# Work behind a rotation, scheduled behind products traced ahead, in a two-layer hybrid block

## The chip, the cores and the metric

One core of one Trainium2 chip runs the whole program. The metric is the device time of one execution in microseconds (us); the figure of a kernel is the median of its runs.

## The reference, cut to what matters

Two layers (`DEPTH = 2`) work on x of 512 tokens by 1024 features. Each layer is this, in float32:

```python
h = rms_norm(x, g_pre_mix)
proj = h @ w_in                      # q, k, v, qi, ki, wi, xr, gr, zu, zv, gate_logits
q = apply_partial_rope(q); k = apply_partial_rope(k)
qi = apply_partial_rope(qi); ki = apply_partial_rope(ki)
y_a = dsa_attention(q, k, v, qi, ki, wi)   # qi, ki, wi score the keys; each query keeps its top 128
xr = causal_depthwise_conv(xr, conv_w, conv_b)
y_b = rg_lru(xr, ...) * gelu(gr)
y_c = chunked_spatial_gating(gelu(zu), rms_norm(gelu(zv), g_gmlp_v), w_spatial, b_spatial)
merged = sum of sigmoid(gate_logits) * (y_n @ w_branch[n]) over n
x = x + rms_norm(merged @ w_out, g_post_mix)
x = x + rms_norm(square(relu(rms_norm(x, g_pre_ffn) @ w_ffn_up)) @ w_ffn_down, g_post_ffn)
x = x + rms_norm((p @ w_ple) * sigmoid(x @ w_ple_gate), g_post_ple)
```

## The kernel before

x lies transposed on the chip, as eight tiles `X0` to `X7` of 128 features by 512 tokens. Every float32 product is made of three products of a narrower type, xh·wh, xh·wl and xl·wh (`mm3`, L297; L356 for the first weights, L590 where tokens stand on the other side), so each operand is first split: a ScalarE cast gives the high part, a subtraction the low part. Weights come in pieces of 128 by 1024 (512 KB) through SyncE's DMA queue: `prep()` (L232) issues the load of `wr`, the cast to `wh` on ScalarE (L243) and the subtraction to `wl` on VectorE (L244). `wh` and `wl` have four buffers each, so a cast also waits until TensorE has done with the piece four back.

The rotation `rope()` (L571) takes a product from PSUM: a multiplication (L573) and a shuffle (L574) on VectorE, a multiplication (L575) and an addition (L576) on GpSimd. Behind it stands a split of its result: `ki_split` for the indexer's key, `stacked` (L645: cast L650 on ScalarE, subtraction L651 on VectorE) for the indexer's four queries `qi0` to `qi3` (tiles `A0` to `A7`) and later for the keys, `q_split` for the attention's queries (L1026 to L1028). `xc_split` (L615) is a split behind the convolution: a cast (L616) and a GpSimd subtraction (L617), four times in a layer (tiles `B0` to `B7`).

The order of the work comes from two places. The program is written by Python code with a clock of its own, `clk`: each product that is written moves it on (`tick`), `defer(us, fn)` writes `fn` once the clock has gone on by `us`, and queues of tasks (indexer, attention) run by it too. A scheduler then orders the instructions of each engine by what they depend on and by where they were written. On the chip each engine takes its instructions strictly in that order. `TURN` (5) is the delay of the splits behind a rotation, `ATT` that of the attention.

Layer one begins on weights that arrive: `FIRST` lists the rows of X at which the pieces of the first three weights (of `xr`, three times eight tiles, 72 products of 512 columns) are cut. Beside them the squares of x are made on ScalarE (L392) and summed into `sacc` on GpSimd (L398), the norm is finished by L408 (sum over partitions on TensorE), L427, L428 (a power on GpSimd), L434 (transposition) and L443. Right behind the 72 products stand the transpositions of the rotation's tables (L163), which need sines (L153, after a load of ScalarE's table) and eight small VectorE instructions (L159, L160). Later norms are made in two halves of 256 tokens, `row(...)`, with the same lines.

Of the kernel before, what the change touches and what calls it, by code (L numbers as in the profile page):

```python
# [12 lines left out]
AF = mybir.ActivationFunctionType  # L13
# [4 lines left out]
S = 512  # L18
D = 1024
KT = 8  # L20
# [20 lines left out]
V_PRE, V_POST, V_FFN, V_PFFN, V_PPLE = 0, 8, 16, 24, 32  # L41
# [9 lines left out]
def hybrid_block_kernel(ctx, tc, xT, pT, pos, vec, bsp, freq, w_in, w_tok, w_lru, w_sp, w_br, w_out, w_up, w_dn, w_ple, w_gate, out, depth=DEPTH, dbg=None):  # L51
    nc = tc.nc
    V, A, G, PE = nc.vector, nc.scalar, nc.gpsimd, nc.tensor
# [13 lines left out]
    def tmp(dt=F32):  # L67
        return tp.tile([128, S], dt, tag="tmp", name=nm("tmp"), bufs=NTMP)
# [11 lines left out]
    FULL = slice(0, S)  # L80
# [7 lines left out]
    TAIL = 3  # L88
    LEAD = 256
    ATT = 13  # L90
    TURN = 5
    WARM = 120
    FIRST = [0, 1, 4]

# [27 lines left out]
    X = [cp.tile([128, S], F32, tag=f"X{k}", name=f"X{k}") for k in range(KT)]  # L124
# [136 lines left out]
    def defer(us, fn):  # L261
        later.append((clk[0] + us, uid[0], fn))
        uid[0] += 1

    def run_later(force=False):
        while later:
# [5 lines left out]
    def add_task(q, gen):  # L272
        q["wait"].append(gen)
# [101 lines left out]
    sacc = cp.tile([128, S], F32, tag="sacc", name="sacc")  # L375

    class Stats:
# [23 lines left out]
        def add(self, src, r=FULL):  # L401
            self.square(src, r)
            self.accumulate(r)
# [33 lines left out]
        def row(self, div, dst):  # L437


            def complete(r):  # L440
                def tok():
                    self.rstd_tok(div, r)
                    defer(3.0, lambda: A.copy(dst[:, r], self.rstd_bc(r)))  # L443

                defer(2.2, tok)

            return complete

# [22 lines left out]
    XS = [(slot(f"xh{k}", F32R), slot(f"xl{k}", F32R)) for k in range(KT)]  # L471

    def x_tiles(r, xs, g=None, st=None, ys=None, bc=None, gp=None, on_g=()):

        def updated(d):
            if ys is not None and d < KT:
                if gp is None:
                    V.tensor_mul(ys[d][:, r], ys[d][:, r], bc)  # L480
                else:
                    V.scalar_tensor_tensor(ys[d][:, r], ys[d][:, r], gp[:, d:d + 1], bc, op0=ALU.mult, op1=ALU.mult)
                (G if d in on_g else V).tensor_add(X[d][:, r], X[d][:, r], ys[d][:, r])  # L483

        updated(0)
        for d in range(KT):
            x = X[d][:, r]
            if xs is not None:
                hi, lo = [v[:, r] for v in xs[d]]
                if g is None:  # L490
                    A.copy(hi, x)
                else:
                    A.activation(hi, x, AF.Copy, scale=g[:, d:d + 1])  # L493
                if st is not None:
                    st.square(x, r)
            updated(d + 1)
            if st is not None:
                st.accumulate(r)
            if xs is not None:
                if g is None:  # L500
                    V.tensor_sub(lo, x, f32v(hi))
                else:
                    V.scalar_tensor_tensor(lo, x, g[:, d:d + 1], f32v(hi), op0=ALU.mult, op1=ALU.subtract)  # L503
            yield d
# [28 lines left out]
    for l in range(depth):  # L533
        vc = vecs[l]
# [5 lines left out]
        if l == 0:  # L540
            st = Stats()

            def gen():
                tiles = x_tiles(FULL, XS, vc[:, V_PRE:V_PRE + 8], st)
                for k in range(KT):
                    first_parts(k)
                    yield next(tiles)

            gen0 = gen()
        else:  # L550
            st = st_next
# [4 lines left out]
        def proj(name, ahead=LA):  # L556
            ps = bank()
            gemm(ps, getw(("in", l, name), ahead), XS, KT)
            return ps
# [11 lines left out]
        def rope(ps, n=128):  # L571
            t1, u = tmp(), tmp()
            V.tensor_mul(t1[:n], ps[:n], Cr[:n])  # L573
            V.stream_shuffle(u[:n], ps[:n], mask=SHUF)  # L574
            G.tensor_mul(u[:n], u[:n], Sr[:n])  # L575
            G.tensor_add(t1[:n], t1[:n], u[:n])  # L576
            return t1
# [19 lines left out]
        idxq = {"wait": [], "act": [], "max": 1}  # L597
# [5 lines left out]
        for j in range(4):  # L603
            ps = first[j]
            xr = tmp()
            V.tensor_mul(xr, ps, R)
            xc = slot(f"M{4 + j}")
            A.activation(xc, xr, AF.Identity, bias=col(V_CB + j), scale=col(V_CW + 12 + j))
            for i in range(3):
                s = 3 - i  # L610
                V.scalar_tensor_tensor(xc[:, s:], xr[:, :S - s], col(V_CW + 4 * i + j), xc[:, s:], op0=ALU.mult, op1=ALU.add)
            xh, xl = slot(f"B{j}", F32R), slot(f"B{4 + j}", F32R)
            XC.append((xc, xh, xl))

            def xc_split(xc=xc, xh=xh, xl=xl):  # L615
                A.copy(xh, xc)  # L616
                G.tensor_sub(xl, xc, f32v(xh))  # L617

            defer(10 + 5 * j, xc_split)


        ps = proj("ki")
# [5 lines left out]
            A.copy(kih[64:128], kf[0:64])  # L628
            A.copy(kil[64:128], f32v(kil[0:64]))

        defer(TURN, ki_split)
        wf = tmp()
        A.copy(wf, ps)
        WI = small(32, "wi", 2).rearrange("p (t h) -> p t h", t=4)
# [5 lines left out]
            for t in range(1, 4):  # L640
                V.tensor_scalar(WI[:, t, :], pw[:, t * 128 + 64:t * 128 + 72], rt[:, t:t + 1], IDX_SCALE, op0=ALU.mult, op1=ALU.mult)

        defer(9, wi_turn)

        def stacked(f, q0, q1):  # L645


            for s, q in enumerate((q0, q1)):
                r, other = slice(64 * s, 64 * s + 64), slice(64 - 64 * s, 128 - 64 * s)
                A.copy(q[r], f[r])  # L650
                V.tensor_sub(q[other], f[r], f32v(q[r]))  # L651
            return q0, q1

        QI = []
        for j in range(4):
            ps = proj(f"qi{j}")
            QI.append((slot(f"A{j}", F32R), slot(f"A{4 + j}", F32R)))
            defer(TURN, lambda f=rope(ps), q=QI[j]: stacked(f, *q))

        def qk(a, b, c, d, jobs):  # L660

# [39 lines left out]
        def indexer():  # L701
            sc = {t: tmp() for t in (1, 2, 3)}
            for t in (1, 2, 3):
                yield from scores(t, sc[t])
            for t in (1, 2, 3):
                yield from select(t, sc[t])
# [23 lines left out]
            G.tensor_scalar(BIAS[t], gt[:, :n], -NEG, NEG, op0=ALU.mult, op1=ALU.add)  # L730
            yield 1.0

        defer(9, lambda: add_task(idxq, indexer()))


        bs = tmp()
# [282 lines left out]
        for j in range(4):  # L1019
            f = rope(proj(f"q{j}"))  # L1020
            q2, ql = (slot(f"A{j}", F32R), slot(f"A{4 + j}", F32R)), tmp(F32R)

            def q_split(f=f, q2=q2, ql=ql):
                for s in range(2):
                    r, other = slice(64 * s, 64 * s + 64), slice(64 - 64 * s, 128 - 64 * s)
                    A.copy(q2[s][r], f[r])  # L1026
                    V.tensor_sub(ql[r], f[r], f32v(q2[s][r]))
                    A.copy(q2[s][other], f32v(q2[s][r]))  # L1028

            defer(TURN, q_split)  # L1030
            Q.append((q2, ql))
            defer(TURN, lambda f=rope(proj(f"k{j}")), j=j: stacked(f, KK[0][:, j], KK[1][:, j]))
            if j == 0:
                finish(idxq)
            defer(ATT, lambda j=j: add_task(attq, attention(j)))
            gated(1, YB, ds=range(2 * j, 2 * j + 2))
# [206 lines left out]
```

## Time and profile before

| | |
|---|---|
| time, median of 3 runs | 1851.07 us (1850.51 to 1853.98) |
| the profiled execution | 1852.94 us, of which the span of instructions is 1851.2 us |
| TensorE (PE) busy | 1803.0 us, 97% of the span |
| VectorE (DVE) busy | 1159.5 us, 63% |
| ScalarE (ACT) busy | 800.3 us, 43% |
| GpSimd (POOL) busy | 361.6 us, 20% |
| DMA | 167.77 MB, 91 GB/s on the average |

The engines are shown as PE, DVE, ACT, POOL and SP; the profile's instruction times overlap a little, since the next instruction starts before the one ahead has quite ended. The idle time that a row gives in brackets is that of its engine just before it, with what ended it. The granted clock is a share of TensorE's full speed.

### The profile page before, as it was taken

The page shows a single profiled execution, that of the slowest core. Times are in us where ns is not written, and L with a number is a line of the kernel's source. Part 1 is how long each engine was busy: PE and PEld are TensorE (multiplying, and loading weights), DVE is VectorE, ACT ScalarE, POOL GpSimd, SP SyncE. Part 2 cuts the span into 40 slices and gives each one's busy share as a digit, 9 for nine tenths or more (in the row PEclk, how much of TensorE's full clock was granted, in tenths as well). Part 3 has the DMA queues.
Part 4 walks back from the last instruction along what each step waited for, and adds up shares of the span by engine and source line. Part 5 has one row for each costly group of instructions (what it writes and reads, how often), then busy time and mean ns, then how long its engine had stood idle before and what let it go on. Part 6 is the DMA issues. An engine that isn't in the chain of part 4 may idle for free.

```text
span 1851.2 us, 22873 instructions
## 1 busy us (share of the span) xinstructions
PE 1803.0 (97%) x8798; PEld 1507.5 (81%) x8798; DVE 1159.5 (63%) x1939; ACT 800.3 (43%) x1292; POOL 361.6 (20%) x292
## 2 busy tenths in 40 slices
PE   8899999999999999999998999999999999999997
PEld 7787887888888888888887878877888888888886
DVE  6689996666386253533685999866563852544355
ACT  5466435664453322223455573455544432222233
POOL 3513212210240000003454141222004200000033
PEclk9999999999999999999999999999999999999999
DMA  5122322222223232332212223222222222222321
GB/s 173 63 92 85 98 92 91 69 80 82 90 80 108 97 98 96 99 106 91 92 58 97 68 92 103 91 80 72 89 80 92 92 92 101 96 97 97 108 80 58
DMA packets 49678, 167.77 MB, mean 91 GB/s; under 512 B 6048, under 2 KB 8864, under 8 KB 49568
## 3 DMA queue, kind: packets, MB, share of 16 engines
q1 hardware_dynamic: 47376, 163.64, 26.8%
q10 hardware_dynamic: 2192, 2.67, 0.4%
q8 instruction: 69, 1.13, 0.3%
q14 instruction: 41, 0.34, 0.1%
HBM read 164.19 MB, written 2.10 MB: 90 GB/s over the span
## 4 chain that ended last, share of the span: by engine, by line
PE 72%; DVE 12%; POOL 6%; issue 6%; ACT 4%; DMA 0%; SPq 0%; POOLq 0%; DVEq 0%; ACTq 0%
PE ps L298 21%; PE ps L299 20%; PE ps L300 20%; PE ps L356 3%; PE ps L590 3%; DVE wl L244 2%; POOL tmp L575 1%; POOL tmp L576 1%; DVE tmp L716 1%; DVE m L714 1%; POOL sacc L398 1%; POOL X L483 1%; PE ps L681 1%; PE ps L967 1%; DVE tmp L790 1%
## 5 line engine op out<-in xcount | busy, mean ns | idle before, releaser
L243 ACT CAST wh<-wr 128x1024 fp32r<-128x1024 f32 x303 | 316.6, 1049 | 453.3 <-PE ps L300 365.9
L244 DVE TENSOR_TENSOR wl<-wr,wh 128x1024 fp32r<-128x1024 f32 x303 | 386.8, 1280 | 188.7 <-ACT wh L243 188.0
L298 PE MATMUL ps<-xh,wh 128*128 128x512 f32 (+1 forms) x1296 | 502.7, 388 | 0.9 <-DVE tmp L370 0.9
L299 PE MATMUL ps<-xh,wl 128*128 128x512 f32 (+1 forms) x1296 | 495.5, 382 | 3.0 <-DVE wl L244 3.0
L300 PE MATMUL ps<-xl,wh 128*128 128x512 f32 (+1 forms) x1296 | 495.6, 382 | 0.0
L398 POOL TENSOR_TENSOR sacc<-sacc,tmp 128x256 f32<-128x256 f32 (+1 forms) x99 | 109.8, 1109 | 894.8 <-issue 584.5
L300 PEld LDWEIGHTS ps<-xl,wh 128*128 128x128 f32 x1296 | 243.9, 188 | 48.2
L299 PEld LDWEIGHTS ps<-xh,wl 128*128 128x128 f32 x1296 | 244.4, 189 | 47.1 <-DVE wl L244 3.9
L298 PEld LDWEIGHTS ps<-xh,wh 128*128 128x128 f32 x1296 | 244.0, 188 | 47.2 <-issue 1.9
L300 PE MATMUL ps<-V,wh 128*128 128x512 f32 (+1 forms) x528 | 195.4, 370 | 0.0
L298 PE MATMUL ps<-K,wh 128*128 128x512 f32 (+1 forms) x432 | 158.2, 366 | 0.0
L299 PE MATMUL ps<-K,wl 128*128 128x512 f32 (+1 forms) x432 | 157.8, 365 | 0.0
L300 PE MATMUL ps<-B,wh 128*128 128x512 f32 x336 | 130.9, 390 | 0.0
L298 PE MATMUL ps<-A,wh 128*128 128x512 f32 x320 | 125.0, 391 | 0.2 <-ACT A L369 0.2
L299 PE MATMUL ps<-A,wl 128*128 128x512 f32 x320 | 124.6, 389 | 0.0
L1102 DVE TENSOR_TENSOR M<-M,ps 128x512 f32<-128x512 f32 x48 | 33.0, 688 | 141.4 <-PE ps L300 141.4
L300 PEld LDWEIGHTS ps<-V,wh 128*128 128x128 f32 x528 | 99.5, 188 | 16.7
L1090 DVE TENSOR_TENSOR tmp<-ps,R 128x512 f32<-128x512 f32 x64 | 43.8, 690 | 108.6 <-PE ps L300 108.5
L356 PE MATMUL ps<-xl,wh 128*128 128x256 f32 (+1 forms) x264 | 88.1, 334 | 6.2 <-DVE xl L503 5.5
L298 PEld LDWEIGHTS ps<-K,wh 128*128 128x128 f32 x432 | 81.5, 189 | 13.3
L299 PEld LDWEIGHTS ps<-K,wl 128*128 128x128 f32 x432 | 81.5, 189 | 13.1
L356 PE MATMUL ps<-xh,wh 128*128 128x256 f32 (+1 forms) x264 | 87.1, 330 | 2.2 <-ACT xh L493 2.2
(237 smaller groups left out, 2733.0 us busy)
## 6 DMA issues: line engine op xcount, KB each, us to landing
wr<-in_w_in_dram SPq DMA_DIRECT2D x95, 512.0 KB, 3.3
wr<-in_w_up_dram SPq DMA_DIRECT2D x64, 512.0 KB, 3.3
wr<-in_w_dn_dram SPq DMA_DIRECT2D x64, 512.0 KB, 3.3
wr<-in_w_br_dram SPq DMA_DIRECT2D x24, 512.0 KB, 3.3
wr<-in_w_tok_dram SPq DMA_DIRECT2D x16, 512.0 KB, 3.3
wr<-in_w_out_dram SPq DMA_DIRECT2D x16, 512.0 KB, 3.3
wr<-in_w_gate_dram SPq DMA_DIRECT2D x16, 512.0 KB, 3.3
X<-in_xT_dram SPq DMA_DIRECT2D x8, 256.0 KB, 5.9
```

The costliest lines, as they stand in the source:

```text
L243: A.copy(hi, raw)
L244: V.tensor_sub(lo, raw, f32v(hi))
L298: PE.matmul(ps, wh, xh, start=start, stop=False)
L299: PE.matmul(ps, wl, xh, start=False, stop=False)
L300: PE.matmul(ps, wh, xl, start=False, stop=stop)
L356: PE.matmul(pss[o][:, r], (h3, l3, h3)[m][:, q], xs[q][m // 2][:, r], start=q == 0 and m == 0, stop=q == KT - 1 and m == 2)
L398: G.tensor_add(sacc[:, r], sacc[:, r], self.q[r.start, r.stop])
L483: (G if d in on_g else V).tensor_add(X[d][:, r], X[d][:, r], ys[d][:, r])
L575: G.tensor_mul(u[:n], u[:n], Sr[:n])
L590: PE.matmul(ps, x, w, start=k == 0 and i == 0, stop=k == KT - 1 and i == 2)
L1090: V.tensor_mul(t, ps, R)
L1102: V.tensor_add(F[d], F[d], ps)
```

## The change

`TURN` goes from 5 to 7; the splits behind a rotation and `xc_split` are deferred through `turn_later`, which also gives each of their ScalarE, VectorE and GpSimd instructions a dependency on the TensorE instruction written last, for the scheduler alone (no wait on a semaphore comes from it). `xc_split` is deferred by 12 + 5j (10 + 5j before), `wi_turn` by 14 (9), the indexer by 12 (9), the end of a norm's first half by 8.0 (2.2). In layer one the squares are written beside the first products, and their sums in two groups of four and three. `FIRST` has one more cut, so X1 and X2 to X3 have pieces of their own (128 and 256 columns wide, in place of 384), three more loads in SyncE's queue, three more casts and three more subtractions.

```diff
-    TURN = 5
+    TURN = 7
     WARM = 120
-    FIRST = [0, 1, 4]
+    FIRST = [0, 1, 2, 4]
...
+    def behind_products(fn):
+        ins = nc.cur_bb.bb.instructions
+        n0 = len(ins)
+        mark = next(i for i in reversed(ins[:n0]) if i.engine == mybir.EngineType.PE)
+        fn()
+        for i in nc.cur_bb.bb.instructions[n0:]:
+            if i.engine in (mybir.EngineType.Activation, mybir.EngineType.DVE, mybir.EngineType.Pool):
+                tc.add_manual_dep(i, mark.name, mybir.DependencyInfo(mybir.DependencyClass.NoSync, mybir.DependencyReason.SCHED_ONLY), reason="behind products")
+
+    def turn_later(us, fn):
+        defer(us, lambda: behind_products(fn))
...
-                defer(2.2, tok)
+                defer(2.2 if r.stop == S else 8.0, tok)
...
-                tiles = x_tiles(FULL, XS, vc[:, V_PRE:V_PRE + 8], st)
+                tiles = x_tiles(FULL, XS, vc[:, V_PRE:V_PRE + 8])
+                qs = []
                 for k in range(KT):
                     first_parts(k)
-                    yield next(tiles)
+                    k = next(tiles)
+                    qs.append(tmp() if k else sacc)
+                    A.activation(qs[k], X[k], AF.Square)
+                    if k in (5, KT - 1):
+                        def add(qs=qs[1:5] if k == 5 else qs[5:]):
+                            for q in qs:
+                                G.tensor_add(sacc, sacc, q)
+                        behind_products(add)
+                    yield k
...
-            defer(10 + 5 * j, xc_split)
+            turn_later(12 + 5 * j, xc_split)
...
-        defer(TURN, ki_split)
+        turn_later(TURN, ki_split)
...
-        defer(9, wi_turn)
+        defer(14, wi_turn)
...
-            defer(TURN, lambda f=rope(ps), q=QI[j]: stacked(f, *q))
+            turn_later(TURN, lambda f=rope(ps), q=QI[j]: stacked(f, *q))
...
-        defer(9, lambda: add_task(idxq, indexer()))
+        defer(12, lambda: add_task(idxq, indexer()))
...
-            defer(TURN, q_split)
+            turn_later(TURN, q_split)
             Q.append((q2, ql))
-            defer(TURN, lambda f=rope(proj(f"k{j}")), j=j: stacked(f, KK[0][:, j], KK[1][:, j]))
+            turn_later(TURN, lambda f=rope(proj(f"k{j}")), j=j: stacked(f, KK[0][:, j], KK[1][:, j]))
```

Where instructions of an engine stand now is seen in its order. The lines of the new file are some 14 to 26 higher: L383 and L384 are L369 and L370 of before, L599 and L600 the rotation's L573 and L574, L642 is L616, L667 is L641, L676 and L677 are L650 and L651.

The first place is on VectorE in layer one, beside the indexer's queries; it stands so in layer two as well. `wl_119`, `wl_129` and `wl_138` are three weights that follow each other, `A0` and `A4` the split of the first query, `A1` and `A5` that of the second. Before:

```order
L244 TENSOR_TENSOR wl_119_654<-wr_117_651,wh_118_653 128x1024
L641 TENSOR_SCALAR wi_105_604<-ps_120_675,rt_37_283 128x8 x3
L573 TENSOR_TENSOR tmp_123_696<-ps_116_650,tmp_73_523 128x512
L651 TENSOR_TENSOR A0_111_642<-tmp_113_644,A0_111_642 64x512
L651 TENSOR_TENSOR A4_112_643<-tmp_113_644,A4_112_643 64x512
L574 STREAM_SHUFFLE tmp_124_697<-ps_116_650 128x512
L244 TENSOR_TENSOR wl_129_706<-wr_127_703,wh_128_705 128x1024
L573 TENSOR_TENSOR tmp_132_741<-ps_126_702,tmp_73_523 128x512
L574 STREAM_SHUFFLE tmp_133_742<-ps_126_702 128x512
L651 TENSOR_TENSOR A1_121_694<-tmp_123_696,A1_121_694 64x512
L651 TENSOR_TENSOR A5_122_695<-tmp_123_696,A5_122_695 64x512
L244 TENSOR_TENSOR wl_138_751<-wr_136_748,wh_137_750 128x1024
```

And after, from the same weight on (`wl_128` is the second weight here):

```order
L244 TENSOR_TENSOR wl_119_657<-wr_117_654,wh_118_656 128x1024
L384 TENSOR_TENSOR M1_102_610<-tmp_99_603,M0_101_609 64x512
L599 TENSOR_TENSOR tmp_122_692<-ps_116_653,tmp_73_532 128x512
L600 STREAM_SHUFFLE tmp_123_693<-ps_116_653 128x512
L244 TENSOR_TENSOR wl_128_702<-wr_126_699,wh_127_701 128x1024
L677 TENSOR_TENSOR A0_111_645<-tmp_113_647,A0_111_645 64x512
L677 TENSOR_TENSOR A4_112_646<-tmp_113_647,A4_112_646 64x512
L667 TENSOR_SCALAR wi_105_613<-ps_129_729,rt_37_286 128x8 x3
L599 TENSOR_TENSOR tmp_132_744<-ps_125_698,tmp_73_532 128x512
L600 STREAM_SHUFFLE tmp_133_745<-ps_125_698 128x512
L244 TENSOR_TENSOR wl_138_754<-wr_136_751,wh_137_753 128x1024
```

Each weight and each rotation now stands one split further ahead: the second weight ahead of A0 and A4, the third ahead of A1 and A5.

The second place is ScalarE in the same stretch, where the casts feed both. Before, from the last cast of `xc_split` on:

```order
L616 CAST B3_92_561<-M7_91_556 128x512
L629 CAST M1_102_601<-M1_102_601 64x512
L243 CAST wh_128_705<-wr_127_703 128x1024
L650 CAST A0_111_642<-tmp_113_644 64x512
L650 CAST A4_112_643<-tmp_113_644 64x512
L243 CAST wh_137_750<-wr_136_748 128x1024
L650 CAST A1_121_694<-tmp_123_696 64x512
L650 CAST A5_122_695<-tmp_123_696 64x512
```

And after:

```order
L243 CAST wh_127_701<-wr_126_699 128x1024
L642 CAST B1_82_552<-M5_81_547 128x512
L655 CAST M1_102_610<-M1_102_610 64x512
L676 CAST A0_111_645<-tmp_113_647 64x512
L676 CAST A4_112_646<-tmp_113_647 64x512
L243 CAST wh_137_753<-wr_136_751 128x1024
L642 CAST B2_87_561<-M6_86_556 128x512
L676 CAST A1_120_690<-tmp_122_692 64x512
L676 CAST A5_121_691<-tmp_122_692 64x512
L243 CAST wh_150_803<-wr_149_801 128x1024
```

The casts B1 to B3 of `xc_split`, which all stood ahead of the splits, now stand between them; so do their subtractions on GpSimd (L617), of which three stood ahead of the key's rotation and one does now.

The third place is ScalarE in layer one behind the arriving products: the sines for the rotation's tables and the first whole weights. Before:

```order
L243 CAST wh_50_412<-wr_49_410 128x1024
L153 ACT_TABLE_LOAD
L153 ACTIVATE tmp_60_436<-tmp_60_436 128x32 x2
L243 CAST wh_53_421<-wr_52_419 128x1024
L243 CAST wh_57_430<-wr_56_428 128x1024
L164 COPY ropeC_234<-ps_62_452 128x512
```

And after:

```order
L243 CAST wh_50_421<-wr_49_419 128x1024
L243 CAST wh_53_430<-wr_52_428 128x1024
L243 CAST wh_57_439<-wr_56_437 128x1024
L153 ACT_TABLE_LOAD
L153 ACTIVATE tmp_60_445<-tmp_60_445 128x32 x2
L243 CAST wh_67_490<-wr_66_488 128x1024
L164 COPY ropeC_234<-ps_62_461 128x512
```

The load of the table and the sines stood ahead of `wh_53` and `wh_57` and stand behind them now. Those two casts need the buffers of the first two arriving weights.

## Rows read from the trace of the kernel before

**Rows 1.** Waits of TensorE: what it waited for, us in total, times, longest us.
```profile
PE ps L590 <- DVE wl L244: 10.5, 4, 4.2
PE ps L356 <- DVE xl L503: 5.5, 9, 2.2
PE ps L299 <- DVE wl L244: 4.4, 4, 1.5
PE ps L967 <- ACT tmp L369: 4.1, 4, 2.3
...
PE ps L967 <- DVE tmp L370: 1.7, 4, 0.9
PE ps L639 <- ACT tmp L633: 1.2, 2, 0.7
```

**Rows 2.** Timeline of TensorE, layer one: start us, us, engine, line, instruction, [idle before].
```profile
72.81 0.39 PE L590 MATMUL ps<-wh,xl 128*128 128x512 f32 x1
...
74.86 0.39 PE L590 MATMUL ps<-wh,xl 128*128 128x512 f32 x1
79.46 0.80 PE L590 MATMUL ps<-wl,xh 128*128 128x512 f32 x1 [4.21 <-DVE wl L244]
...
84.23 0.40 PE L590 MATMUL ps<-wh,xl 128*128 128x512 f32 x1
```

**Rows 3.** Timeline of VectorE in the same stretch.
```profile
68.86 1.41 DVE L651 TENSOR_TENSOR A<-tmp,A 64x512 fp32r<-64x512 f32 x2 [3.45 <-ACT A L650]
...
75.38 2.76 DVE L651 TENSOR_TENSOR A<-tmp,A 64x512 fp32r<-64x512 f32 x2 [1.93 <-ACT A L650]
78.18 1.23 DVE L244 TENSOR_TENSOR wl<-wr,wh 128x1024 fp32r<-128x1024 f32 x1
```

**Rows 4.** Timeline of ScalarE in the same stretch.
```profile
68.21 1.26 ACT L650 CAST A<-tmp 64x512 fp32r<-64x512 f32 x2 [3.87 <-POOL tmp L576]
69.49 1.05 ACT L243 CAST wh<-wr 128x1024 fp32r<-128x1024 f32 x1
74.73 1.26 ACT L650 CAST A<-tmp 64x512 fp32r<-64x512 f32 x2 [4.18 <-POOL tmp L576]
```

**Rows 5.** Timeline of GpSimd in the same stretch.
```profile
59.39 1.28 POOL L576 TENSOR_TENSOR tmp<-tmp,tmp 64x512 f32<-64x512 f32 x1
...
71.00 2.33 POOL L575 TENSOR_TENSOR tmp<-tmp,tmp 128x512 f32<-128x512 f32 x1 [2.83 <-DVE tmp L574]
```

**Rows 6.** Windows: stretch, length, busy of PE, PEld, DVE, ACT, POOL, clock, DMA.
```profile
100.00:120.00 20.00, 20.00 (x93) 16.92 (x92) 16.85 (x52) 15.55 (x28) 2.12 (x2) 1.00 0.30 103
200.00:220.00 20.00, 19.34 (x86) 15.69 (x85) 19.73 (x35) 6.16 (x9) 1.29 (x1) 1.00 0.33 106
980.00:1000.00 20.00, 14.76 (x55) 11.36 (x54) 12.42 (x18) 5.80 (x8) 12.15 (x9) 0.83 0.32 104
```

**Rows 7.** Timeline of ScalarE, VectorE and TensorE, behind the arriving products.
```profile
21.62 1.28 ACT L153 ACT_TABLE_LOAD   x1
28.88 0.35 ACT L153 ACTIVATE tmp<-tmp 128x32 f32<-128x32 f32 x2 [5.97 <-DVE tmp L152]
30.70 2.00 ACT L243 CAST wh<-wr 128x1024 fp32r<-128x1024 f32 x2 [1.47 <-issue]
...
29.49 0.17 DVE L159 TENSOR_SCALAR tmp<-tmp 128x32 f32<-128x32 f32 x1
...
31.82 1.04 PE L163 MATMUL ps<-ident,tmp 128*128 128x128 f32 x8
```

**Rows 8.** Timeline of VectorE and GpSimd, beside the arriving products.
```profile
15.46 5.19 DVE L370 TENSOR_TENSOR wl<-wr,wh 128x512 fp32r<-128x512 f32 x3
...
16.99 6.47 POOL L398 TENSOR_TENSOR sacc<-sacc,tmp 128x512 f32<-128x512 f32 x4 [0.30 <-ACT tmp L392]
```

**Rows 9.** Timeline of TensorE: a norm's first half, and attention in layer two.
```profile
531.71 0.43 PE L434 MATMUL ps<-ident,rt 128*128 128x128 f32 x2 [0.37 <-POOL rt L428]
...
1212.28 1.04 PE L967 MATMUL ps<-tmp,V 128*128 128x256 f32 x4 [2.35 <-ACT tmp L369]
```

## The prediction

> **What bounds the kernel now.** TensorE does: it is busy for 97% of the span, so only what it waits for, and what it runs slowly, can be won. I read first the list of TensorE's waits [rows 1], which names the releaser and the number of times: most of what it waits for late in the program is a weight's subtraction (L244) or a cast or subtraction of the attention. Then the timelines of the four engines around the longest of these waits [rows 2 to 5], to see why the weight was late; then windows [rows 6], to see where VectorE has room to catch up and where the clock falls; then the same around the starts [rows 7, 8].
>
> In the stretch at 75 us, nine products from 72.81 to 74.86 us take 0.228 us each. The twelve steps from 74.86 to 84.23 us take 9.37 us where 2.73 would do: 6.64 us lost, 4.21 idle and 2.4 in slow steps behind it [rows 2]. In layer two's copy of it the granted clock is 0.83 over 20 us [rows 6]: part of it at the 1.2 GHz level after 4.2 idle us, the rest at 2.4. The weight that TensorE waits for was cast by 70.54 us [rows 4], but its subtraction starts at 78.18, behind the split of the second query (A1, A5), which starts at 75.38 after a wait for ScalarE [rows 3]; ScalarE had waited 4.18 us for GpSimd's addition [rows 4]. GpSimd had itself waited 2.83 us for a shuffle [rows 5], which stood on VectorE behind the first query's split, itself held up by 3.45 us [rows 3]. So work that was ready (a weight) stands behind work that was not (a rotation's end), twice in each layer.
>
> **The change, part by part.**
>
> *Splits behind a rotation.* In the new order the weight stands ahead of the split that held it. I take the times of before as a bound. The key's addition on GpSimd ends at 60.67 [rows 5]; two casts and a weight's cast later (two of 0.63, half of the pair of 1.26, and 1.05 [rows 4]) it is 63.0, so that the second weight is subtracted (1.23 [rows 3]) by about 64.3. TensorE asks for it near 71. The third weight's cast stays behind A0 and A4, at 70.54; VectorE then has only those two (until 70.27) and, as an estimate, at most 3.2 us of rotation ahead, the time in which it did as much between 70.27 and 73.45 (75.38 less its wait of 1.93) [rows 3]. It ends near 74.7. TensorE asked at 75.25 (79.46 less 4.21), now about 1 us sooner. That is a near thing by GpSimd's old times, but these improve: three of the four subtractions L617 stood ahead of the key's rotation and one does now, and the second query's shuffle comes before the second weight, some 6 us sooner. I therefore count all of it as gone, in both layers: the four waits of 10.5, the two of 1.2 for the transposition behind L633, which `wi_turn` now writes later (both [rows 1]), and twice 2.4 of slow steps: **−16.5 us**. Bounds: a fourth weight that comes late, below, gives 12 back.
>
> What is late next? VectorE is busy 16.85 of 20 us at 100 to 120, so it follows TensorE there and carries no backlog into what comes after; at 200 to 220 it is busy 19.73 [rows 6].
>
> *Later weights of the same layers.* The other four waits for weights, 4.4 us [rows 1], are two a layer, behind the indexer's queries. The new order puts the first weight there ahead of the LRU's VectorE work and defers the third behind it. VectorE's whole work stays the same, and it has next to no idle time until 220, so what is won before 200 is mostly asked for again by 220 [rows 6]. **−2.0**, bounds 0 and −4.4.
>
> *Attention.* A cast for the probabilities (L369) stood behind the splits of the next query, as at 1212.28 [rows 9], and stands ahead of them now, on both engines. These waits are 4.1 and 1.7 us in all [rows 1], and slow steps follow the longest. Some latency stays, since TensorE goes from a transposition to this product at once: **−4.5**, bounds 0 and −7.5 (5.8, and 1.7 for slow steps after a wait half as long as that of [rows 2]).
>
> *First half of a norm.* Its transposition waited 0.37 us [rows 9], once in each layer; it is written 50 to 80 products later now, and what reads it later has the second half to wait for anyway: **−0.7**, bounds −1.5 and +1.
>
> *Finer first pieces.* X1 has 384 KB less ahead of it in SyncE's queue, so TensorE's second batch of products starts sooner. But VectorE ends the stretch: it makes three subtractions in 5.19 us beside GpSimd's sums [rows 8], where the wait for `xl` then follows (the longest, 2.2 [rows 1]). Three subtractions more, a quarter of that size each, are 3 × 1.73 / 4 = 1.3 us at that rate, and their wider partners are smaller by as much. I take 0, bounds −1 and +1.3. The two groups of squares I cost at nothing: the order has the seven additions where they were, each waiting for its own square; GpSimd's idleness hides them, and a rival prices the contrary.
>
> *The sines.* This one goes the other way. ScalarE loaded its table at 21.62 and made the sines at 28.88, ahead of two weight casts that had to wait for buffers until 30.70 [rows 7]. Now the sines stand behind these casts: 30.70 + 2.00 + 1.28 + 0 puts them at 33.98. The fifth of the eight VectorE instructions began 0.61 after the sines did (29.49 less 28.88), so the table's transpositions can begin near 34.65, not 31.82 [rows 7]. Nothing else stands on TensorE in between: behind those transpositions are queued all the products of the next weight, although it is ready. +2.8, and slow steps behind an idle time of that length, between 0 and 2.4 [rows 2], of which I take 2.0, since the engine also has small transpositions there: **+4.8**, bounds +2.8 and +5.2.
>
> The table's load takes 1.28 us in that row. The Trainium skill ("ScalarE: Activation LUTs", What ACT_TABLE_LOAD costs) gives the same for the load but adds a drain of about 1.38 us to each switch of tables. By the page this term would be +6.2 and the time 1833; these rows do not show what follows a load directly, since the sines waited for VectorE.
>
> Sum: −16.5 − 2.0 − 4.5 − 0.7 + 0 + 4.8 = **−18.9**. From the profiled execution's own 1852.94 (1851.2 of span and 1.7 around it) that is 1834.0; this execution lies 1.9 above the median, so from the median of 1851.07 it is **1832**.
>
> **The rivals.**
>
> *A. A wait takes the place of the one removed.* The fourth weight's cast now stands behind A1's and A5's. By the old times these casts end at 75.99, the weight's at 77.04, and with the split (2.76) and 2.6 for a rotation and the weight itself VectorE is done at 80; TensorE would ask near 76.3, 7.9 before 84.23. That is 3.7 of wait and 2.4 of slow steps a layer, 12 in all: **1844**. For it: only GpSimd's earlier additions prevent it. Against it: the shuffle that held the additions back is now 6 us sooner.
>
> *B. VectorE becomes the bound.* If its stretch from 140 to 240 did not move forward with TensorE, the gains ahead of it would come back as waits for weights: of 16.5 + 2.0 nothing is left, −4.5 − 0.7 + 4.8 = −0.4, **1851**. For it, 19.73 busy of 20; against it, the idle time at 100 to 120 [rows 6]. Half of it gives 1841.
>
> *C. The sines cost nothing*, because the casts find their buffers earlier: 1832 − 4.8 = **1827**. Against it: the buffers are freed by the arriving products themselves, 1.1 us before the transpositions.
>
> *D. The two groups do hold the sums back.* Then VectorE is undisturbed until the sixth tile, and the wait of 2.2 and its slow steps go, about −4: **1828**. Against it: the order.
>
> *E. Slower.* GpSimd's subtractions now lie between the rotations, beside VectorE's weights. Two splits took 1.41 undisturbed and 2.76 beside GpSimd [rows 3], so a disturbed weight may cost 1.2 more. A weight feeds 24 products, 5.5 us by [rows 2], so the 120 us from 140 to 260 hold some 22. From eight more of them disturbed in each layer while VectorE is full, 19.2 are lost and the kernel is slower; with fifteen, 36, and it is at **1868**. Against it: GpSimd has as many instructions as before, and those of that stretch do not move into it. The Trainium skill speaks for the mechanism ("GPSIMD Engine Reference", 1. Specifications): GpSimd shares its SBUF interfaces with VectorE, with contention where VectorE's instruction has two SBUF inputs, as every subtraction here has. The rows agree, with the pair of 1.41 and 2.76.
>
> **How the numbers follow.** Forecast 0.53; A 0.12; B half 0.12, whole 0.06; C 0.07; D 0.05; E 0.05. Anything within 0.2% (3.7 us) cannot be told from no change. Faster: 0.53 + 0.12 + 0.12 + 0.07 + 0.05 = 0.89; same, B whole, 0.06; slower, E, 0.05. For the range I go on the good side to C with the later weights in full and half of the attention's rest (1832 − 4.8 − 2.4 − 1.5 = 1823), on the other to A: **1823 to 1844**, which leaves out B whole, E and a little beyond both ends.
>
> **What would show it.** Right: no wait of TensorE on L244's successor at 70 to 85 us and 915 us later, clock 1.00 there; a wait of about 2.8 us ahead of L163's successor near 32 us, released by VectorE behind ScalarE's sines, with slow steps after it. Wrong: a wait for the fourth weight (A), waits for weights at 177 to 240 that sum to more than 4.4 (B), L163 starting at 32 (C), GpSimd's first addition long after the first square (D), weights' subtractions longer on the mean than the 1.23 of [rows 3] in more places than before (E).

## The result: half the gain that was forecast

The changed kernel took 1840.32 us, the median of 4 runs (1838.18 to 1843.74), beside 1850.85 for the kernel before in the same runs. The ratio is 0.9941, with a 95% interval of 0.9922 to 0.9960: faster by 10.5 us, where 1832 stood in the forecast (18.9 faster). The range of 1823 to 1844 holds it. The profiled execution took 1840.19 us, of which the span is 1838.5: 12.7 less than before.

The page's busy times, and the list of TensorE's waits (what it waited for, us in total, times, longest), of the changed kernel:

```profile
PE 1799.8 (98%) x8798; PEld 1507.8 (82%) x8798; DVE 1172.6 (64%) x1942; ACT 795.6 (43%) x1291; POOL 369.2 (20%) x292
```

```profile
PE ps L313 <- DVE wl L244: 9.5, 5, 3.3
PE ps L370 <- DVE xl L518: 6.2, 10, 1.9
PE ps L616 <- DVE wl L244: 3.9, 2, 2.0
PE ps L163 <- DVE tmp L160: 2.8, 1, 2.8
```

L616 is the old L590, L313 the old L299, L370 the old L356. Beside [rows 1], the four waits of 10.5 us behind the rotation have become two of 3.9, the attention's waits (L967 before, L993 now) and that of the transposition behind `wi` (L639) are gone, and two things are worse: a wait for the sines (L163) that was not there, and waits for weights at L313 of 9.5 us where 4.4 stood.

**Where the time went.** The waits alone miss slow steps, products that TensorE starts 0.427 us apart behind a wait, at the lower clock, and not 0.227. So I took TensorE's timeline in both profiles and subtracted the start of the first product with the same weight, all along the program. The sums of this difference by stage (us; the places are times in the kernel before):

| stage | forecast, both layers | after | delay alone (e4) | indexer at 9 (e1) | also sines, fourth weight (e6) |
|---|---|---|---|---|---|
| arriving weights, to 50.45 | +4.8 | +2.19 | +0.79 | +0.16 | −3.50 |
| layer one: rotation, to 130.88 | −16.5 | −6.53 | −0.20 | −6.57 | −8.73 |
| layer one: later weights, to 231.78 | −2.0 | +4.92 | +4.98 | +0.07 | −0.03 |
| layer one: attention, to 386.98 | −4.5 | −5.69 | −1.10 | −5.71 | −5.71 |
| to 964.95 | −0.7 | +0.23 | +0.22 | +0.69 | +0.64 |
| layer two: rotation, to 1045.62 | above | −6.60 | +1.13 | −5.06 | −8.97 |
| layer two: later weights, to 1143.79 | above | +4.96 | +4.96 | +0.04 | +0.02 |
| layer two: attention, to 1302.91 | above | −6.42 | −3.32 | −5.35 | −5.38 |
| to the end | | +0.28 | +0.30 | +0.32 | +0.31 |
| sum | −18.9 | −12.66 | +7.76 | −21.41 | −31.35 |

The sums agree with the differences of the spans, one profile of each kernel. The last three columns belong to experiments below. One row is far off the wrong way: the later weights, forecast to give 2.0 in all, cost 4.9 in each layer.

**The later weights.** VectorE's timeline of the changed kernel (start us, us, engine, line, instruction, [idle before]); L895 are the LRU's subtractions (L869 before), L244 the three weights:

```profile
168.52 1.49 DVE L244 TENSOR_TENSOR wl<-wr,wh 128x1024 fp32r<-128x1024 f32 x1 [2.44 <-ACT wh L243]
172.26 1.77 DVE L895 SCALAR_TENSOR_TENSOR B<-tmp,B 128x512 f32<-128x512 f32 x1 [2.26 <-POOL tmp L894]
...
174.48 1.53 DVE L244 TENSOR_TENSOR wl<-wr,wh 128x1024 fp32r<-128x1024 f32 x1
175.93 1.53 DVE L895 SCALAR_TENSOR_TENSOR B<-tmp,B 128x512 f32<-128x512 f32 x1
...
178.50 1.66 DVE L895 SCALAR_TENSOR_TENSOR B<-tmp,B 128x512 f32<-128x512 f32 x1
...
180.56 0.67 DVE L895 SCALAR_TENSOR_TENSOR B<-tmp,B 128x512 f32<-128x512 f32 x1
...
183.52 1.22 DVE L244 TENSOR_TENSOR wl<-wr,wh 128x1024 fp32r<-128x1024 f32 x1
```

GpSimd in the same stretch:

```profile
171.18 1.04 POOL L894 TENSOR_TENSOR tmp<-B 128x512 f32<-128x512 f32 x1
...
173.44 4.92 POOL L894 TENSOR_TENSOR tmp<-B 128x512 f32<-128x512 f32 x3
```

ScalarE's casts of the second and third weight:

```profile
169.54 1.05 ACT L243 CAST wh<-wr 128x1024 fp32r<-128x1024 f32 x1
...
176.32 1.03 ACT L243 CAST wh<-wr 128x1024 fp32r<-128x1024 f32 x1
```

And TensorE, in layer one and in layer two:

```profile
181.12 0.39 PE L312 MATMUL ps<-xh,wh 128*128 128x512 f32 x1
184.79 0.80 PE L313 MATMUL ps<-xh,wl 128*128 128x512 f32 x1 [3.28 <-DVE wl L244]
...
1092.39 0.79 PE L313 MATMUL ps<-xh,wl 128*128 128x512 f32 x1 [3.28 <-DVE wl L244]
```

The second weight is cast by 170.59, while VectorE stands idle for 2.26 us until GpSimd's first L894 ends; it is subtracted at 174.48, behind the first L895. The third is cast by 177.35, on ScalarE behind activations of the LRU, and subtracted at 183.52: it stands behind all four of L895 and, between them, steps of the indexer, which VectorE works off without a pause from 172.26 on. TensorE stands still for 3.28 us from 181.5 and goes on in slow steps, 2.92 us more. The idle VectorE ahead of a ready weight is the forecast's own picture of the rotation, work that is ready behind work that is not, 100 us further on. How much of the third weight's delay is that lost time, and how much the order behind it, the runs don't separate.

**The rotation.** VectorE's timeline beside the indexer's queries, with the weights (L244) and the splits (L677):

```profile
67.19 3.37 DVE L677 TENSOR_TENSOR A<-tmp,A 64x512 fp32r<-64x512 f32 x2
...
72.24 1.81 DVE L244 TENSOR_TENSOR wl<-wr,wh 128x1024 fp32r<-128x1024 f32 x1
74.08 3.37 DVE L677 TENSOR_TENSOR A<-tmp,A 64x512 fp32r<-64x512 f32 x2
...
78.71 1.21 DVE L244 TENSOR_TENSOR wl<-wr,wh 128x1024 fp32r<-128x1024 f32 x1
```

ScalarE ahead of the last of these weights, then TensorE:

```profile
71.74 0.62 ACT L676 CAST A<-tmp 64x512 fp32r<-64x512 f32 x1 [2.35 <-POOL tmp L602]
...
73.03 1.06 ACT L243 CAST wh<-wr 128x1024 fp32r<-128x1024 f32 x1
```

```profile
79.97 0.50 PE L616 MATMUL ps<-wl,xh 128*128 128x512 f32 x1 [1.87 <-DVE wl L244]
```

The third weight is subtracted at 72.24 and TensorE no longer waits for it. The fourth (78.71) stands behind A1's and A5's split, which takes 3.37 us beside GpSimd (2.76 in [rows 3], and 1.41 for the pair that ran undisturbed there), and behind the next rotation's two instructions. Its cast was done by 74.09, so without the split in between it should have been in time; e6 below tests that. This is rival A, at a third of its price.

**The sines.** ScalarE, VectorE and TensorE behind the arriving products, which end at 28.2 (31.8 before):

```profile
26.99 2.00 ACT L243 CAST wh<-wr 128x1024 fp32r<-128x1024 f32 x2 [6.01 <-PE ps L370]
29.01 1.28 ACT L153 ACT_TABLE_LOAD   x1
30.30 0.35 ACT L153 ACTIVATE tmp<-tmp 128x32 f32<-128x32 f32 x2
```

```profile
13.99 2.98 DVE L384 TENSOR_TENSOR wl<-wr,wh 128x512 fp32r<-128x512 f32 x3
...
30.56 0.18 DVE L159 TENSOR_SCALAR tmp<-tmp 128x32 f32<-128x32 f32 x1
```

```profile
31.15 1.94 PE L163 MATMUL ps<-ident,tmp 128*128 128x128 f32 x8 [2.83 <-DVE tmp L160]
```

The wait is the one forecast, 2.83 us against 2.8, with 2.28 us of slow steps behind it. But the arriving products ended 3.7 us sooner, which the forecast had at nothing. The three subtractions of VectorE beside them took 2.98 us where they took 5.19 [rows 8].

The windows of the changed kernel (stretch, length, busy of PE, PEld, DVE, ACT, POOL, clock, DMA) show where TensorE is now at the lower of its two levels for part of the time, 1.2 GHz instead of 2.4:

```profile
30.00:40.00 10.00, 8.85 (x35) 7.56 (x36) 2.61 (x11) 2.75 (x6) 1.03 (x1) 0.66 0.53 159
70.00:90.00 20.00, 18.13 (x84) 14.81 (x83) 18.06 (x22) 10.93 (x17) 12.23 (x8) 1.00 0.21 66
175.00:195.00 20.00, 16.72 (x62) 13.30 (x61) 19.54 (x28) 11.71 (x15) 12.28 (x8) 0.83 0.25 79
970.00:1000.00 30.00, 27.98 (x128) 22.93 (x127) 25.82 (x30) 18.05 (x27) 19.70 (x12) 1.00 0.29 93
```

The rotation's stretches are at 1.00 (0.83 in layer two before [rows 6]); 175 to 195 is at 0.83 and the stretch behind the sines, from 30 to 40, at 0.66.

### The profile page after: what moved, and what is told of

The parts are those of the page before. It is cut to its first block, busy times and chain, and to the rows that moved or that the text cites. A ratio compares the mean times of both kernels' runs of the same rounds, so it can differ in the third digit from the quotient of the medians.

```text
span 1838.5 us, 22885 instructions
## 1 busy us (share of the span) xinstructions
PE 1799.8 (98%) x8798; PEld 1507.8 (82%) x8798; DVE 1172.6 (64%) x1942; ACT 795.6 (43%) x1291; POOL 369.2 (20%) x292
## 3 DMA queue, kind: packets, MB, share of 16 engines
q8 instruction: 69, 1.13, 0.3%
## 4 chain that ended last, share of the span: by engine, by line
PE 80%; DVE 8%; POOL 5%; issue 3%; ACT 3%; SPq 0%; DMA 0%; ACTq 0%; POOLq 0%; DVEq 0%
PE ps L312 23%; PE ps L314 23%; PE ps L313 23%; PE ps L616 4%; PE ps L370 3%; DVE wl L244 1%; PE ps L993 1%; DVE tmp L742 1%; PE ps L979 1%; POOL X L498 1%; DVE m L740 1%; PE ps L707 1%; POOL sacc L412 1%; POOL tmp L601 1%; DVE M L637 1%
## 5 line engine op out<-in xcount | busy, mean ns | idle before, releaser
L244 DVE TENSOR_TENSOR wl<-wr,wh 128x1024 fp32r<-128x1024 f32 x303 | 384.9, 1272 | 192.6 <-ACT wh L243 192.3
L313 PE MATMUL ps<-xh,wl 128*128 128x512 f32 (+1 forms) x1296 | 498.1, 384 | 9.5 <-DVE wl L244 9.5
L313 PEld LDWEIGHTS ps<-xh,wl 128*128 128x128 f32 x1296 | 245.7, 190 | 55.6 <-DVE wl L244 12.0
L412 POOL TENSOR_TENSOR sacc<-sacc,tmp 128x256 f32<-128x256 f32 (+1 forms) x92 | 99.2, 1078 | 884.9 <-issue 584.1
L313 PE MATMUL ps<-K,wl 128*128 128x512 f32 (+1 forms) x432 | 157.8, 365 | 0.0
L313 PE MATMUL ps<-A,wl 128*128 128x512 f32 x320 | 124.5, 389 | 0.0
L370 PE MATMUL ps<-xl,wh 128*128 128x256 f32 (+1 forms) x264 | 87.9, 333 | 6.9 <-DVE xl L518 6.2
L313 PEld LDWEIGHTS ps<-K,wl 128*128 128x128 f32 x432 | 81.5, 189 | 13.1
L370 PE MATMUL ps<-xh,wh 128*128 128x256 f32 (+1 forms) x264 | 86.0, 326 | 0.0
```

The costliest lines, as they stand in the source:

```text
L244: V.tensor_sub(lo, raw, f32v(hi))
L313: PE.matmul(ps, wl, xh, start=False, stop=False)
L370: PE.matmul(pss[o][:, r], (h3, l3, h3)[m][:, q], xs[q][m // 2][:, r], start=q == 0 and m == 0, stop=q == KT - 1 and m == 2)
L412: G.tensor_add(sacc[:, r], sacc[:, r], self.q[r.start, r.stop])
```

## The experiments

Ratios are to the kernel before in the same runs, with 95% intervals; the changed kernel stands at 0.9941. All start from the changed kernel.

**e1_idx9: the indexer's delay back at 9.**

```diff
-        defer(12, lambda: add_task(idxq, indexer()))
+        defer(9, lambda: add_task(idxq, indexer()))
```

> The changed kernel with the indexer started 9 behind the key's rotation again, as before the change, in place of 12. In the order this puts the three weights behind the LRU's first activations side by side again, where the change had put the third behind four subtractions of the LRU. Theory 1 (what stands ahead of a weight in an engine's order decides): the two waits of 3.28 us for that third weight, the slow steps behind them and the wait of 1.49 us in layer two go, and at most the 1.5 and 0.7 us a layer of the kernel before are left there; some 8 to 10 us less, 1831. Theory 2 (VectorE is full from 140 to 240 us and asks back what TensorE won at 70 to 85): waits for weights in that stretch still sum to over 9 us, wherever they stand, and the time stays at 1838 to 1842.

Measured: 1832.4 us (1831.44 to 1835.2), ratio 0.9896 [0.9881, 0.9911]. VectorE's timeline:

```profile
166.94 1.75 DVE L895 SCALAR_TENSOR_TENSOR B<-tmp,B 128x512 f32<-128x512 f32 x1 [1.23 <-POOL tmp L894]
...
170.99 0.68 DVE L895 SCALAR_TENSOR_TENSOR B<-tmp,B 128x512 f32<-128x512 f32 x1
171.59 4.34 DVE L244 TENSOR_TENSOR wl<-wr,wh 128x1024 fp32r<-128x1024 f32 x3
175.85 1.53 DVE L895 SCALAR_TENSOR_TENSOR B<-tmp,B 128x512 f32<-128x512 f32 x1
```

The windows of 160 to 180 us, of the changed kernel and then of e1 (busy of PE, PEld, DVE, ACT, POOL, clock, DMA):

```profile
160.00:180.00 20.00, 20.00 (x90) 16.54 (x90) 13.64 (x22) 17.23 (x22) 13.86 (x11) 1.00 0.17 56
160.00:180.00 20.00, 18.44 (x81) 14.94 (x80) 17.58 (x29) 17.23 (x23) 11.43 (x9) 1.00 0.25 80
```

Theory 1. The three weights stand together behind two subtractions, as they did before the change, and the table's later weights go from +4.92 and +4.96 to +0.07 and +0.04. So an order that one number sets lost 9.8 us in the profile, 8 in the median. A full VectorE (rival B) did not: e1's is the fuller one, 17.58 of these 20 us against 13.64, and has no such loss. What the rotation won stays won, but for 1.5 us of slow steps in layer two (a clock of 0.94 from 970 to 1000). The L163 wait grew to 4.5 us because the arriving products ended 2.3 us sooner here, with the clock at 1.00 from 16 to 26 us where the changed kernel had 0.83; the sines held the start all the same.

**e2_sines: the table load and the sines ahead of the second and third whole weight.**

```diff
+                sines_at.append(nc.cur_bb.bb.instructions[-1].name)
...
+            for i in casts[1:3]:
+                tc.add_manual_dep(i, sines_at[-1], mybir.DependencyInfo(mybir.DependencyClass.NoSync, mybir.DependencyReason.SCHED_ONLY), reason="behind the sines")
```

> The changed kernel, with the table load and the two sines ahead of the second and third whole weight's cast on ScalarE in layer one, by a dependency for the scheduler alone. Theory 1 (that order is what the wait of 2.83 us ahead of the table's transpositions comes from): that wait and the 2.3 us of slow steps go, the two casts come 0.7 us later, 1835. Rival (the win is asked back at the next late weight): the wait goes and the time stays within 2 us of 1840, with more waits for weights at 77 or at 181 us.

Measured: 1836.29 us (1835.9 to 1838.42), ratio 0.9914 [0.9897, 0.993]. In its profile the wait at L163 is gone, but the arriving products ended at 30.7: the subtractions beside GpSimd took longer again (VectorE, the row that took 2.98 above), TensorE waited 3.0 us for `xl` behind them (1.9 in the changed kernel), and its clock was 0.66 from 16 to 26 us.

```profile
14.23 4.07 DVE L389 TENSOR_TENSOR wl<-wr,wh 128x512 fp32r<-128x512 f32 x3
```

The ratio fell by 0.27%, 5 us, about the forecast's +4.8 for the sines taken back; with the two intervals overlapping, this alone doesn't prove the size. The profile shows 1.8 us of it; it is of the slowest of the four runs. e5 tries it again.

**e3_first: the arriving weights in pieces as before.**

```diff
-    FIRST = [0, 1, 2, 4]
+    FIRST = [0, 1, 4]
```

> The changed kernel with the first weights in the three pieces of before. In the order the sines then stand ahead of the two casts again. Theory 1 (the finer pieces made the arriving products end 3.7 us sooner, and the same edit moved the sines): the arriving products end near 31.6 us as before the change, with no wait behind them; the start is 1.2 us shorter than with the change and the kernel at 1839. Rival (the squares' sums in two groups gave VectorE room): the arriving products end near 28 us all the same, and with the sines ahead the kernel is at 1835.

Measured: 1838.71 us (1835.18 to 1840.27), ratio 0.9925 [0.991, 0.994], not told apart from the changed kernel. VectorE, ScalarE and TensorE:

```profile
15.38 5.17 DVE L384 TENSOR_TENSOR wl<-wr,wh 128x512 fp32r<-128x512 f32 x3
```

```profile
21.38 1.28 ACT L153 ACT_TABLE_LOAD   x1
28.78 0.35 ACT L153 ACTIVATE tmp<-tmp 128x32 f32<-128x32 f32 x2 [6.12 <-DVE tmp L152]
```

```profile
31.52 0.39 PE L370 MATMUL ps<-xl,wh 128*128 128x512 f32 x1
31.75 1.03 PE L163 MATMUL ps<-ident,tmp 128*128 128x128 f32 x8
```

These are [rows 7, 8] again, within 0.3 us. So the one cut does both: it ends the arriving products sooner and, by the order, it puts the sines behind two casts. No difference of the medians is left that could be told from none.

**e4_nodep: the longer delays without the dependency.**

```diff
     def turn_later(us, fn):
-        defer(us, lambda: behind_products(fn))
+        defer(us, fn)
```

> The changed kernel with the splits deferred by the same amounts, but without the scheduler's dependency on the TensorE instruction written last. On ScalarE the casts of the second query's split then stand ahead of the third weight's cast, and those of the convolution ahead of the key's. Theory 1 (the dependency, not the longer delay, puts a weight ahead of a split): the waits at 70 to 85 us come back at 3 to 6 us a layer with slow steps behind the longer, 1847 to 1853. Rival (a TURN of 7 alone does it): 1838 to 1842, and no wait there above the 2 us that the change left.

Measured: 1860.61 us (1859.04 to 1862.54), ratio 1.0046 [1.0031, 1.0061], slower than before the change. TensorE's waits and ScalarE's timeline:

```profile
PE ps L616 <- ACT wh L243: 5.0, 4, 1.5
PE ps L616 <- DVE wl L244: 4.0, 4, 1.5
```

```profile
69.54 1.26 ACT L676 CAST A<-tmp 64x512 fp32r<-64x512 f32 x2 [4.06 <-POOL tmp L602]
...
72.49 1.25 ACT L676 CAST A<-tmp 64x512 fp32r<-64x512 f32 x2 [1.04 <-POOL tmp L602]
73.77 1.04 ACT L243 CAST wh<-wr 128x1024 fp32r<-128x1024 f32 x1
```

The third weight's cast (73.77) stands behind both splits and waits with them for GpSimd's additions. Of the rotation's 13.1 us nothing is left, of the attention's 12.1 us 4.4. The dependency makes the gain, the delays alone don't; the dependency with the old delays was not run, so whether it needs the longer ones is open. The later weights cost the same 5.0 here as with it, which also puts that loss on the indexer's delay, which both have.

**e5_both: the indexer at 9 and the sines ahead** (the diffs of e1 and e2).

> The changed kernel with the indexer's delay back at 9 (as in e1_idx9) and the table load with its two sines ahead of the second and third whole first weight (as in e2_sines). Theory 1 (two independent losses of order): the third late weight of layer one (3.28 us in the changed kernel) and TensorE's wait for the sines (4.5 us in e1_idx9, 2.8 in the changed kernel) are both gone, and e1_idx9's 1832.4 falls by 3 to 4.5 us: 1828 to 1829.5. Theory 2 (what the sines cost comes back elsewhere while x arrives, as in e2_sines, where the arriving products ended as late as before the change): 1831.5 to 1833.

Measured: 1828.22 us (1827.4 to 1829.08), ratio 0.9877 [0.9863, 0.989]. Theory 1 by the time. The wait for the sines was not gone but fell to 1.5 us, and the first product behind the arriving ones came at 28.48, 2.7 sooner than in the changed kernel. The two losses of order about add up (0.45% in e1 and 0.27% in e2): 0.64% under the changed kernel, 12 us.

**e6_fourth: also the second pair's split behind the fourth weight.**

```diff
+        lows.append(nc.cur_bb.bb.instructions[-1])
+        while held:
+            i = held.pop(0)
+            w = casts[-1] if i.engine == mybir.EngineType.Activation else lows[-1]
+            tc.add_manual_dep(i, w.name, mybir.DependencyInfo(mybir.DependencyClass.NoSync, mybir.DependencyReason.SCHED_ONLY), reason="behind a weight")
...
+        def behind_weight(j, fn):
+            n0 = len(nc.cur_bb.bb.instructions)
+            fn()
+            if j == 1:
+                held.extend(nc.cur_bb.bb.instructions[n0:])
...
-            turn_later(TURN, lambda f=rope(ps), q=QI[j]: stacked(f, *q))
+            turn_later(TURN, lambda f=rope(ps), q=QI[j], j=j: behind_weight(j, lambda: stacked(f, *q)))
```

> e5_both with the second head pair's split (both ScalarE casts and both VectorE subtractions) put behind the fourth weight after the rotation on both engines. Theory 1 (the fourth weight is late because this split stands ahead of it): the two waits for that weight's low part, 1.87 us in layer one and 2.02 in layer two of the changed kernel, are gone, 3.5 to 4 us under e5_both. Theory 2 (VectorE has no room there, the fifth weight or the attention's first scores ask the time back): within 1 us of e5_both.

Measured: 1821.69 us (1821.24 to 1821.97), ratio 0.9841 [0.9828, 0.9854], 6.5 us under e5, more than theory 1 gave. VectorE's timeline, and TensorE's window:

```profile
66.56 1.80 DVE L249 TENSOR_TENSOR wl<-wr,wh 128x1024 fp32r<-128x1024 f32 x1
...
69.53 1.20 DVE L249 TENSOR_TENSOR wl<-wr,wh 128x1024 fp32r<-128x1024 f32 x1
70.77 8.21 DVE L689 TENSOR_TENSOR A<-tmp,A 64x512 fp32r<-64x512 f32 x6
```

```profile
970.00:1000.00 30.00, 30.00 (x143) 25.40 (x142) 26.06 (x40) 23.19 (x42) 9.77 (x7) 1.00 0.31 106
```

The fourth weight (69.53) now follows the third, and three splits run behind it without TensorE asking for them. TensorE is busy for all 30 us; before the change it was for 14.76 of the last 20 of them [rows 6]. The rotation gives 8.73 and 8.97 us, 17.7 in all. That e6 won more on e5 than the 4 us of waits is layer two's slow steps: in e5 the wait of 2.0 us there had them behind it, with a clock of 0.94 from 970 to 1000, and here it is 1.00.

**e7_squares: the squares summed one by one, as before.** (The tiles' loop gets `st` back; the grouped additions go.)

> The changed kernel with layer one's squares accumulated one by one on GpSimd as before the change. Theory 1 (the grouping moves only GpSimd's work, which TensorE doesn't wait for; rival D of the prediction at nothing): within 1.5 us of the changed kernel, 1839 to 1842. Theory 2 (the gaps that the grouping leaves on GpSimd are what made VectorE's three subtractions beside the arriving products take 2.98 us instead of 5.19, and the arriving products end at 27.9 instead of 31.6): these come back, the wait for the sines goes with them, and the first weights' products end 2 to 4 us later, 1841 to 1843.

Measured: 1840.07 us (1838.78 to 1843.58), ratio 0.9949 [0.9935, 0.9962]. Theory 1: the grouping does nothing that is measured. VectorE and GpSimd:

```profile
13.89 2.98 DVE L384 TENSOR_TENSOR wl<-wr,wh 128x512 fp32r<-128x512 f32 x3
```

```profile
16.47 6.60 POOL L412 TENSOR_TENSOR sacc<-sacc,tmp 128x512 f32<-128x512 f32 x4 [1.35 <-ACT tmp L406]
```

The subtractions take 2.98 us here too, in the same gap of GpSimd. The gap comes with the finer pieces, not with the grouping: here GpSimd was idle for 1.35 us ahead of that row, and in e3, grouped but with the old pieces, for 0.28. The pieces let VectorE start at 13.9 and not 15.46 [rows 8], ahead of GpSimd's longest run of additions, which starts between 16.5 and 17 either way.

**e8_xc: only the convolved halves' splits deferred as before.**

```diff
-            turn_later(12 + 5 * j, xc_split)
+            defer(10 + 5 * j, xc_split)
```

> The changed kernel with the convolved halves' splits (L642) deferred as before the change, by 10 instead of 12 and without the dependency; the rotation's own splits keep theirs. Theory 1 (the 20 us that e4_nodep lost are the rotation's splits standing ahead of the weights): 1840 to 1843. Theory 2 (the convolved halves' casts stand ahead of the key's split and the following weights, and it is they that hold the weights back): 1847 or more, with waits for ScalarE's weight cast in the second whole product after the rotation.

Measured: 1846.05 us (1844.46 to 1848.91), ratio 0.9976 [0.9967, 0.9985]; between the two theories. About 6.5 of the 19.4 us that e4 lost against the changed kernel are these splits'. TensorE waited 6.5 us for weights at L616, in four pieces, instead of 3.9 in two, and the rotation's two stages gave 3.3 and 3.4 us instead of 6.5 and 6.6. All four waits were for VectorE's low part, none for ScalarE's cast, as theory 2 had it.

## Why the prediction was right or wrong

**Right by range and side, in part by luck.** The mechanism, a weight that is ready behind a split that is not, twice a layer, is the rotation's gain: with the dependency alone taken out (e4), all of it goes. That the time lies in the range rests on two misses that went opposite ways: the later weights came out 11.9 us worse than forecast, the attention 7.6 better. Without the second the time would be near 1848, outside. It also lies by the 1841 of rival B's half, whose mechanism e1 excludes.

**The step that failed: "Later weights of the same layers", −2.0 with bounds 0 and −4.4.** It measured +9.9 over both layers. The step saw the third weight deferred behind the LRU's VectorE work, and then argued from VectorE's total: the work stays the same, so at most the gains are asked back. But VectorE doesn't work through what it is given; it waits in order. At the first L895 it stood idle for GpSimd while a cast weight lay ready behind. And it was not full up to 220: [rows 6] show 16.85 of 20 us busy from 100 and 19.73 from 200, and between them, from 160 to 180, it was 17.47 before, which the prediction didn't look at; the change made it 13.64, and the third weight, behind all four of L895, came 3.28 us too late in each layer. e1 settles it: a fuller VectorE, no loss. The same question that was asked of the rotation (what stands ahead of this weight, and what does that wait for?) would have found it in the order.

**The rotation, −16.5.** It measured −13.1 (−6.5 and −6.6). The third weight came in time, as forecast. The fourth did not, and rival A's mechanism was right where its price was not: 1.87 and 2.02 us of wait with the clock at 1.00, not 3.7 with 2.4 of slow steps. With that split out of the way (e6) the term is −17.7, so the forecast's −16.5 is about what two punctual weights are worth; its argument, GpSimd's additions come sooner, carried the third weight and not the fourth, since what held that one was VectorE's pair of splits, 3.37 us.

**Attention, −4.5.** It measured −12.1 in the table's stages, which hold more than the products the term spoke of; the waits at L993 are all gone, also the rest that the forecast left standing. It went beyond even the term's bound of −7.5. By the two profiles, 6.7 of it are idle time (5.8 of [rows 1] and 0.9 ahead of a product at L298), 1.7 are slow steps in layer two (a clock of 0.99 over that stage before, 1.00 after), and 3.6 lie in the steps into and among the products of L993 themselves, in gaps too short for the list of waits, which the term left out.

**First half of a norm, −0.7.** Nothing won: +0.2 and +0.3 in the table's quiet stages. Its two waits are gone from the list (L448 has one wait of 1.7 where L434 had three of 2.5), but up to 964.95 TensorE waited 0.5 us more for `xl` at L370.

**Finer first pieces, 0.** In the profile −3.7 at the end of the arriving products. The step assumed that the three subtractions stay beside GpSimd's additions; part of them moved into a gap between these. How much of that a median holds was not settled: with the same pieces the products ended anywhere from 25.4 (e4) to 30.7 (e2, where the subtractions took 4.07), and as long as the sines stand behind the casts an early end brings nothing, since L163 started between 30.1 and 31.2 in every such run.

**The sines, +4.8.** 2.83 of wait and 2.28 of slow steps make +5.1. Most of it could be avoided by the order (e5). Rival C falls: the casts did find their buffers 3.7 us earlier, but the products ended as much earlier, and the wait stayed. The sine starts 1.29 us after its table load does, and the load 0.02 after the cast ahead of it ends. The drain of about 1.38 us that the Trainium skill ("ScalarE: Activation LUTs", What ACT_TABLE_LOAD costs) adds to each switch of tables is not seen in these rows, and the term went by the rows rightly.

**The other rivals.** B fell with e1, D with e7. E asked for more weights at a higher price; the mean of a weight's subtraction is 1.27 us in the changed kernel and was 1.28 before, so nothing of E is seen there, but the pairs of splits did lengthen.

## What to carry to other kernels

When work is deferred on engines that run strictly in order, look at every place where the new order sets an operand that is ready behind an instruction that waits for another engine, also far from the place that the change is about; a sum of busy time doesn't show it. A delay and a scheduler's dependency are not the same: here the delays alone lost 0.46% and with the dependency they won 0.59%. Single numbers (a delay, a list of cuts) moved unrelated work by one place and cost 5 to 10 us, so put orders that matter down as dependencies, as e6 does with two of them (the third it mends by a delay): it is 29.7 us faster than the kernel before, with the same arithmetic.

## What the hardware showed unexpectedly

A wait of the same length was followed by different clocks. After the 2.83 us at L163 the changed kernel's TensorE had a granted clock of 0.66 from 30 to 40 us. In e7, after a wait of 2.8 there, it was 1.00:

```profile
30.00:40.00 10.00, 8.97 (x50) 7.69 (x51) 2.79 (x12) 3.91 (x8) 1.03 (x1) 1.00 0.46 159
```

Both had been at 0.83 from 16 to 26, with a wait of about 2 us there. So the cost of slow steps behind a wait of 2.83 us was 2.28 us in one execution and nothing in another, and one profile shows one of them; the runs don't say what decides.
